# Lengths, lags and per-head shifts of a list schedule for attention, and twelve places for the value tiles

## The chip, the core and the metric

One core of a Trainium2 chip runs the whole kernel. Its engines are TensorE (PE in the profile, with PEld for its weight loads), VectorE (DVE), ScalarE (ACT), GpSimd (POOL) and SyncE (SP), which issues most of the DMAs. The metric is the device time of one execution in microseconds (us); several runs of a kernel are told by their median.

## The reference, cut to what matters

The kernel computes one layer of a transformer for 512 latent tokens and 256 context tokens: modulated RMS norms, two attention mixers side by side, an output projection and a gated feed-forward. The change lies in the attention. Its two mixers, eight heads each, are:

```python
def _diff_attend(q, k, v, lam):
    q1, q2 = jnp.split(q, 2, axis=-1)
    k1, k2 = jnp.split(k, 2, axis=-1)
    s1 = jnp.einsum('bhqd,bhkd->bhqk', q1, k1).astype(jnp.float32) * DA_SCALE
    s2 = jnp.einsum('bhqd,bhkd->bhqk', q2, k2).astype(jnp.float32) * DA_SCALE
    w = jax.nn.softmax(s1, axis=-1) - lam * jax.nn.softmax(s2, axis=-1)
    return jnp.einsum('bhqk,bhkd->bhqd', w.astype(v.dtype), v)

def _softmax_attend(q, k, v, scale):
    s = jnp.einsum('bhqd,bhkd->bhqk', q, k).astype(jnp.float32) * scale
    p = jax.nn.softmax(s, axis=-1)
    return jnp.einsum('bhqk,bhkd->bhqd', p.astype(v.dtype), v)
```

The first (differential attention) takes its queries, keys and values straight from the input projection `h @ w_in`. The second (latent attention) takes them from two normed latents, `c_q @ w_uq` and `c_kv @ w_ukv`. Keys and values come from all 768 tokens, queries from the 512 latent ones. The result of the first is normed per head, and both go through `w_o`.

## The kernel before, in words

All products are made of three matmuls each (helper `mm3`, lines 226 to 231): each operand is held as a rounded high part and the rest as a low part, and high x high, high x low and low x high are summed in PSUM. So every weight block and every intermediate is split: ScalarE casts the high part, VectorE subtracts it to get the low part (`split`, `parts`, `block`).

The stages in order of time are: norms and modulation; the input projection (features, then values); attention; the output projection; the feed-forward; the final norm.

**Values.** Lines 613 to 628 compute the values of all heads in two halves of 512 columns. Six PSUM tiles per half (`vo`, four in the two `s` tiles and two in `b` tiles) collect the products of sixteen k tiles. Each is then split into the tiles kh and kl of the pool `kvs`, two buffers for each tag, and stored to DRAM (`v_d`), by SP's queue in the first half and by POOL's in the second. In this stage the framework orders the instructions of the engines, and a gemv for the modulation (`next_gemv`) runs beside the products.

**Attention** is a flow (class `Flow`, line 73). Each piece of work is a `step` with an engine, a cost, a due time `at` and the buffers that it reads and writes; `lag` is the time from its end until another engine can use its result. `Flow.run` is a list scheduler: it goes through modelled time, and whenever an engine is free it takes, of the steps whose inputs are there and whose ring buffers are free, the one with the smallest `at`. Rings hand out their buffers in the order of `at`. The order found is then written out by hand for PE, ACT, DVE, SP and POOL; each engine executes its own list in order, and semaphores hold an instruction back until its inputs are there. The model's times have no other effect than this order.

- `SPANS` and `BASE` (742, 743) are the planned length and begin of the 16 heads, eight of each mixer, in us from the begin of attention.
- `da_feature` (808) makes the next head's queries: sixteen `mm3` into the tile f, the rotary embedding (`turned`) and the scaled split (`stacked`). Its weights come by `block` (652): a load by SP (`fetch`, 640) into a ring `wr` of three, due 14 before use, the cast `wh` and the rest `wl`. `hx_open` (892) follows the last feature.
- `scores` (686): four or ten matmuls into one of two `s` tiles, the negated row maximum `m` (DVE), exp into `p` with its sum (ACT).
- `weighted_values` (705): transposes of the weights (pt), their split into wth and wtl, and the product with the values in po.
- `load_keys`, `load_values`, the store of a head's output (`o_d`) and the weight blocks all go through SP's one queue.
- In the first mixer POOL scales the second softmax map and adds it to the first (841, 844).
- `open_latents` (868) frees the modulated input and loads the latents `cn` and the rotary key `krh` for the second mixer. `head_queries`, `head_keys`, `head_value` and `rotary_queries` make its operands; `sub_norm` (948) is the per-head norm of the first mixer's outputs, run beside the second.
- From line 1068 the first quarter of the output projection is in the same flow, so that it can stand among the last head's steps.

The pools `kv` and `kvs` of the projection are released before `dp` and `da` of attention are opened in the same SBUF. Lines 747 to 751 make some tiles ahead, to fix where the rings lie and with which buffer they begin.

The scheduler's lines on lags and choice:

```python
    LAGS = {"PE": 0.25, "ACT": 0.07, "DVE": 0.07, "POOL": 0.1, "SP": 3.5, "X": 0.0}
...
                    s = min(can, key=lambda s: (s.at, s.n))
```

Of the kernel before, what the change touches and what calls it, by code (L numbers as in the profile page):

```python
# [17 lines left out]
P = 128  # L18
D = 2048
KT = D // P  # L20
# [51 lines left out]

class Flow:


    LAGS = {"PE": 0.25, "ACT": 0.07, "DVE": 0.07, "POOL": 0.1, "SP": 3.5, "X": 0.0}

    def __init__(self):
        self.steps, self.rings = [], {}
# [6 lines left out]
    def step(self, eng, cost, at, fn, r=(), w=(), needs=(), lag=None):  # L86
        s = Step(eng, cost, self.LAGS[eng] if lag is None else lag, at, fn, len(self.steps))
# [22 lines left out]
    def run(self):  # L110
# [4 lines left out]
        engines = {e: now if e == "SP" else -3.0 for e in self.LAGS}  # L115
# [25 lines left out]
        event(-3.0)  # L141
# [36 lines left out]
def layer_kernel(ctx: ExitStack, tc: tile.TileContext, small, rope, c_row, cc_row, x_t, ctx_t, ada, ada_k,  # L178
# [457 lines left out]
    flow = Flow()  # L636
# [3 lines left out]
    def fetch(t, src, cols, lag=4.0):  # L640
# [8 lines left out]
        step("SP", 0.1 * len(src), t - 14, load, w=[raw], lag=lag)  # L649
        return raw  # L650

    def block(t, *src):
# [5 lines left out]
        step("ACT", 0.12 + cols * 0.00091, t - 4, lambda: sc.copy(hi()[:, :cols], raw()[:, :cols]), r=[raw], w=[hi])  # L658
        step("DVE", 0.15 + cols * 0.00104, t - 2.8, lambda: ve.tensor_tensor(
# [7 lines left out]
    def parts(t, hl, src, dst, of, scale=None, w=0.6, gap=0.7):  # L667
# [15 lines left out]
        step("DVE", w + 0.09, t + gap, second, r=[src, hl[0]], w=[hl[1]])  # L683


    def scores(t, cost, mms, reads, p, l, lcol, extra=None):
# [4 lines left out]
        def mm():  # L691
            ms = mms()
            for c0, c1 in ((0, T), (T, TT)):
# [4 lines left out]
        step("DVE", 0.95, t + cost + 0.2, lambda: ve.tensor_reduce(out=m(), in_=s()[:, :TT], axis=AX.X, op=ALU.max,  # L698
                                                                   negate=True), r=[s], w=[m])
        step("ACT", 1.1, t + cost + 1.3, lambda: sc.activation(p(), s()[:, :TT], AF.Exp, bias=m(), accum_out=lcol()),  # L700
             r=[s, m], w=[p, l])
# [3 lines left out]
    def weighted_values(t, pace, ws, v, vr, dst, after=None):  # L705

        po = buf(lambda: b_tile("po", 1), "po", 1)
        for kt in range(NKEY):
# [8 lines left out]
            step("PE", 0.44, t0, turn, r=ws, w=[pt])  # L717
            parts(t0 + 0.6, wt, pt, lambda b: b(), lambda pt=pt: pt())
            step("PE", 0.69, t0 + 2.5, lambda wt=wt, kt=kt: mm3(po(), v(kt), [b() for b in wt], kt == 0,
                                                                 kt == NKEY - 1), r=[*wt, *vr(kt)], w=[po])  # L720
        step("ACT", 0.6, t + pace * 5 + 3.4, lambda: sc.copy(dst(), po()), r=[po], w=[dst])
# [28 lines left out]
    da.tile([P, T], F32, tag="rt", name=nm("rt"), bufs=2)  # L750
    b_tile("pt", 2)
    zeroed = [buf(lambda t=t: t) for t in klz]
    for n_, (t, b) in enumerate(zip(klz, zeroed)):
        for i, r in enumerate((hi, lo)):
            step("SP", 0.1, FIRST + 3 * n_, lambda t=t, i=i, r=r: nc.sync.dma_start(t[r, i].bitcast(F32), zero_d), w=[b])
# [6 lines left out]
    def first_queries():  # L762
        qs = [da_buf([P, T], F32R, f"qs{i}", 2) for i in range(2)]
        for i in range(2):
            step("SP", 0.1, FIRST + 1, lambda i=i: nc.sync.dma_start(qs[i]().bitcast(F32), q0_d[i]), w=[qs[i]], lag=8.0)
        queries[0] = qs

    def load_keys(t, h):
# [7 lines left out]
        step("SP", 0.4, t, load, w=[ks, kl], lag=4.0 if h else 8.0)  # L776
        keys_[h] = ks, kl

    def load_values(t, h):
# [6 lines left out]
        step("SP", 0.2, t, load, w=hl)  # L786
        wvals[h] = hl

    def turned(t, src, tmp):

        q, u = tmp(), tmp()
        step("DVE", 0.69, t, lambda: ve.tensor_tensor(q(), src(), ropet[:, 0, :], op=ALU.mult), r=[src], w=[q])
        step("DVE", 0.75, t + 0.7, lambda: ve.stream_shuffle(u(), src(), mask=[i ^ 16 for i in range(32)]), r=[src],
             w=[u])
        step("DVE", 0.8, t + 1.5, lambda: ve.tensor_tensor(u(), u(), ropet[:, 1, :], op=ALU.mult), w=[u])
        step("DVE", 0.75, t + 2.3, lambda: ve.tensor_tensor(q(), q(), u(), op=ALU.add), r=[u], w=[q])
        return q

    def stacked(t, q, make, scale):
        qs = [make(i) for i in range(2)]  # L800
        for i, (r, o) in enumerate(((lo, hi), (hi, lo))):
            step("ACT", 0.63, t + 0.7 * i, lambda i=i, r=r: sc.mul(qs[i]()[r], q()[r], scale), r=[q], w=[qs[i]])
            step("DVE", 0.73, t + 0.7 * i + 0.8, lambda i=i, r=r, o=o: ve.scalar_tensor_tensor(
# [4 lines left out]
    def da_feature(f0, pace, h, blocks):  # L808
        f = buf(lambda: b_tile("f", 1), "f", 1)
        for kt in range(KT):  # L810
# [4 lines left out]
            step("PE", 0.69, f0 + pace * kt, mm, r=[*blocks[kt // 8], hx_open], w=[f])  # L815
# [14 lines left out]
    for h in range(NH):  # L830
        b, pace = BASE[h], SPANS[h] / 8
        ws = []
        for qt in range(NQT):
            ps = [weights_tile(), da_buf([P, TT], F32, "p1", 3)]
            l, rl = small("l", 2), small("rl", 2)
            for i in range(2):
# [3 lines left out]
            step("DVE", 0.17, t, lambda l=l, rl=rl: ve.reciprocal(rl(), l()), r=[l], w=[rl])  # L840
            step("POOL", 1.15, t + 0.2, lambda p=ps[1], rl=rl: gp.tensor_scalar(
                out=p(), in0=p(), scalar1=rl()[:, 1:2], scalar2=neglam, op0=ALU.mult, op1=ALU.mult), r=[rl], w=[ps[1]])
            step("ACT", 0.95, t + 0.2, lambda p=ps[0], rl=rl: sc.mul(p(), p(), rl()[:, 0:1]), r=[rl], w=[ps[0]])
            step("POOL", 1.9, t + 1.5, lambda ps=ps: gp.tensor_tensor(out=ps[0](), in0=ps[0](), in1=ps[1](),
                                                                      op=ALU.add), r=[ps[1]], w=[ps[0]])
            ws.append(ps[0])
        load_values(b + 2, h)
# [9 lines left out]
        hl = wvals[h]  # L857
        weighted_values(BASE[h + 1] + 4.0, 3.05, ws, lambda kt, hl=hl: [g()[:, kt * P:(kt + 1) * P] for g in hl],
# [959 lines left out]
```

## Time and profile before

| | |
|---|---|
| median of 3 runs | 2418.42 us (2418.08 to 2422.07) |
| the profiled execution, own time | 2417.74 us |
| its span, first to last instruction | 2416.0 us |
| mean granted TensorE clock | 0.994 |
| PE waits between 425 and 860 us | 18.3 us |

A row of the timeline has the start (us from the begin of the span), the length, engine, line, operation, the tile that is written and those that are read, the count, and in brackets how long the engine had been idle before it and what released it. In waits, the columns are the total, how often, and the longest. PE's lengths are modelled and overlap, since matmuls are pipelined; the pitch of two matmuls is read from their starts. A wait of an engine is idle time that ended with the event named.

### The profile page before, as it was taken

What the parts mean: (1) busy time and instruction counts of PE and PEld (TensorE: products, weight loads), DVE (VectorE), ACT (ScalarE), POOL (GpSimd) and SP (SyncE); (2) the same over time, 40 slices, a digit from 0 to 9 for tenths busy, and PEclk for the clock granted to TensorE, in tenths of its full rate; (3) what the DMA queues carried; (4) which work ended last, traced back from release to release, by engine and by line L of the source; (5) the groups of instructions that cost most, each with busy time, mean ns of one, the idle gap of its engine ahead of it and who ended that gap; (6) DMA issues with size and microseconds to landing.
All of it is one profiled execution on the core that took longest, in us unless ns stands there. A gap on an engine that the chain in (4) does not pass through costs nothing.

```text
span 2416.0 us, 33008 instructions
## 1 busy us (share of the span) xinstructions
PE 2345.0 (97%) x12758; PEld 1980.2 (82%) x12758; DVE 1698.2 (70%) x2244; ACT 1154.3 (48%) x1752; POOL 334.8 (14%) x320
## 2 busy tenths in 40 slices
PE   6999999999999999999999999999999999999998
PEld 3678888787788878888888888888888888888887
DVE  6668886387877777289575757676767676676667
ACT  4333121176776732255454545454544454554545
POOL 0000000154432222100101010101010111111110
PEclk9999999999999999999999999999999999999999
DMA  8867888734511168423555555555565656555563
GB/s 290 287 225 291 317 341 318 254 112 121 180 64 50 36 232 325 135 85 113 140 139 140 136 143 130 146 125 151 120 157 122 157 122 155 125 143 137 135 188 105
DMA packets 132852, 404.31 MB, mean 167 GB/s; under 512 B 14627, under 2 KB 25379, under 8 KB 124243
## 3 DMA queue, kind: packets, MB, share of 16 engines
q1 hardware_dynamic: 106166, 351.66, 44.0%
q0 software_dynamic: 25376, 49.49, 11.6%
q8 instruction: 100, 1.64, 0.3%
q10 hardware_dynamic: 1152, 1.05, 0.1%
q14 instruction: 58, 0.48, 0.1%
HBM read 332.47 MB, written 69.67 MB: 166 GB/s over the span
## 4 chain that ended last, share of the span: by engine, by line
PE 70%; issue 16%; DVE 6%; ACT 3%; DMA 2%; POOL 2%; SPq 0%; DVEq 0%; POOLq 0%; ACTq 0%
PE b L230 8%; PE b L229 8%; PE b L231 8%; PE y L1537 8%; PE z L1537 4%; PE y L1539 4%; PE s L229 4%; PE s L231 4%; PE s L230 4%; PE s L695 3%; PE z L1539 2%; POOL x_d L1558 2%; PE x L1537 1%; PE pt L715 1%; PE f L229 1%
## 5 line engine op out<-in xcount | busy, mean ns | idle before, releaser
L1558 POOL DMA_DIRECT2D x_d<-xs x160 | 139.8, 1003 | 1160.5 <-ACT xs L1557 1158.4
L1393 DVE TENSOR_TENSOR wl<-wr,wh 128x1024 fp32r<-128x1024 f32 x144 | 176.4, 1225 | 157.1 <-ACT wh L1385 156.5
L1385 ACT CAST wh<-wr 128x1024 fp32r<-128x1024 f32 x144 | 150.8, 1048 | 233.3 <-PE b L230 118.1
L229 PE MATMUL b<-ah,wh 128*128 128x512 f32 (+1 forms) x664 | 257.1, 387 | 0.0
L230 PE MATMUL b<-al,wh 128*128 128x512 f32 (+1 forms) x664 | 257.0, 387 | 0.0
L231 PE MATMUL b<-ah,wl 128*128 128x512 f32 (+1 forms) x664 | 256.2, 386 | 0.0
L1393 DVE TENSOR_TENSOR wl<-rb,wh 128x1024 fp32r<-128x1024 f32 x123 | 150.0, 1220 | 126.9 <-ACT wh L1385 126.9
L1385 ACT CAST wh<-rb 128x1024 fp32r<-128x1024 f32 x123 | 129.3, 1051 | 185.1 <-PE b L230 116.2
L1393 DVE TENSOR_TENSOR wl<-ws,wh 128x1024 fp32r<-128x1024 f32 x123 | 150.1, 1220 | 90.0 <-ACT wh L1385 90.0
L1385 ACT CAST wh<-ws 128x1024 fp32r<-128x1024 f32 x123 | 128.3, 1043 | 130.3 <-DVE ws L1347 44.5
L297 DVE CUSTOM_DVE_ANT_0 ada<-ada,cb,smt 128x2048 f32<-128x2048 f32 x64 | 152.1, 2381 | 40.7 <-DMA ada<-in_ada 40.4
L1537 PE MATMUL y<-a2k,wh 128*128 128x512 f32 x656 | 164.0, 392 | 0.0
L205 ACT CAST wh<-wr 128x1024 fp32r<-128x1024 f32 (+1 forms) x69 | 67.5, 978 | 178.8 <-PE b L231 76.3
L229 PE MATMUL b<-a2k,wh 128*128 128x512 f32 (+1 forms) x376 | 141.6, 377 | 5.9 <-ACT a2k L1242 4.3
L231 PEld LDWEIGHTS b<-ah,wl 128*128 128x128 f32 x664 | 124.9, 188 | 25.7
L229 PEld LDWEIGHTS b<-ah,wh 128*128 128x128 f32 x664 | 125.1, 188 | 22.8
L230 PEld LDWEIGHTS b<-al,wh 128*128 128x128 f32 x664 | 125.1, 188 | 21.9
L230 PE MATMUL b<-a2k,wh 128*128 128x512 f32 (+1 forms) x376 | 140.8, 374 | 0.0
L231 PE MATMUL b<-a2k,wl 128*128 128x512 f32 (+1 forms) x376 | 139.9, 372 | 0.0
L1537 PEld LDWEIGHTS y<-a2k,wh 128*128 128x128 f32 x656 | 118.7, 189 | 21.5
L206 DVE TENSOR_TENSOR wl<-wr,wh 128x1024 fp32r<-128x1024 f32 (+1 forms) x69 | 80.1, 1161 | 52.5 <-ACT wh L205 52.0
L698 DVE TENSOR_REDUCE m<-s 128x1 f32<-128x768 f32 x96 | 90.9, 950 | 28.1 <-PE s L695 27.9
(458 smaller groups left out, 5931.0 us busy)
## 6 DMA issues: line engine op xcount, KB each, us to landing
ada<-in_ada SPq DMA_DIRECT2D x64, 1024.0 KB, 6.2
rb<-in_w_up SPq DMA_DIRECT2D x123, 512.0 KB, 4.3
wr<-in_w_dn SPq DMA_DIRECT2D x88, 512.0 KB, 4.2
x_d<-xs POOLq DMA_DIRECT2D x160, 256.0 KB, 5.9
wr<-in_w_up SPq DMA_DIRECT2D x53, 512.0 KB, 4.2
wr<-in_w_f SPq DMA_DIRECT2D x34, 512.0 KB, 7.3
ada<-in_ada SPq DMA_DIRECT2D x32, 512.0 KB, 7.3
adak<-in_ada_k SPq DMA_DIRECT2D x32, 512.0 KB, 6.1
```

The lines of the kernel that those rows point to most:

```text
L206: ve.tensor_tensor(dst_l, src, dst_h.bitcast(F32), op=ALU.subtract)
L229: pe.matmul(out, st[0], mv[0], start=start, stop=False, **kw)
L230: pe.matmul(out, st[0], mv[1], start=False, stop=False, **kw)
L231: pe.matmul(out, st[1], mv[0], start=False, stop=stop, **kw)
L297: ve.tensor_tensor_reduce(out=junk, in0=w, in1=vec, op0=ALU.mult, op1=ALU.add, scale=1.0, scalar=col("b_ada", j), accum_out=dst[:, j:j + 1])
L695: pe.matmul(s()[:, c0:c1], a, b[:, c0:c1], start=i == 0, stop=i == len(ms) - 1)
L698: step("DVE", 0.95, t + cost + 0.2, lambda: ve.tensor_reduce(out=m(), in_=s()[:, :TT], axis=AX.X, op=ALU.max, negate=True), r=[s], w=[m])
L1385: sc.copy(t, raw[:, k * n_:k * n_ + n_])
L1393: ve.tensor_tensor(t, raw[:, k * n_:k * n_ + n_], hi[k].bitcast(F32), op=ALU.subtract)
L1537: pe.matmul(o, w[j][0], hs[j], start=start and j == 0, stop=False, skip_group_check=True)
L1539: pe.matmul(o[:, h0], w[j][1], hs[j][:, h0], start=False, stop=j == 7, skip_group_check=True)
L1558: gp.dma_start(x1_d[dt], x, accum_op=ALU.add)
```

## The change

It has two parts.

**Lengths, lags and shifts.** All costs in the flow are set anew, most a little shorter, POOL's longer, and DMA issues from 0.1 us apiece to about 0.4 to 0.6. The lag of a load goes from 3.5 or 4.0 to 6.0, and loads are due 16 instead of 14 before use. A table `PLAN` shifts the due times of named groups of steps: s0 to s15 are the scores of the 16 heads, f1 to f7 a head's loads and the next head's features, w0 to w15 the weighted values, m the second mixer's queries and keys, v its values, n the sub-norms, x the opening of pools, o the projection. Due times of the features and of the latents' loads move, and the engines begin at different times.

```diff
+PLAN = {
+    "f1": -1.5, "f2": -3.2, "f3": -0.3, "f4": 1.2, "f5": -0.3, "f6": -2.3, "f7": -20.4, "m-1": 2.0, "m0": 3.2,
...
+    0.2, "w12": -2.7, "w13": 2.2, "w14": 0.3, "w15": 10.3, "x": 4.8}
...
-    LAGS = {"PE": 0.25, "ACT": 0.07, "DVE": 0.07, "POOL": 0.1, "SP": 3.5, "X": 0.0}
+    LAGS = {"PE": 0.2, "ACT": 0.14, "DVE": 0.14, "POOL": 0.1, "SP": 6.0, "X": 0.0}
...
     def step(self, eng, cost, at, fn, r=(), w=(), needs=(), lag=None):
+        at += self.plan.get(self.part, 0.0)
...
-        engines = {e: now if e == "SP" else -3.0 for e in self.LAGS}
+        engines = {"PE": -3.0, "ACT": 2.0, "DVE": 2.8, "POOL": 0.0, "SP": now, "X": -3.0}
...
-    def fetch(t, src, cols, lag=4.0):
+    def fetch(t, src, cols, lag=6.0):
...
-        step("SP", 0.1 * len(src), t - 14, load, w=[raw], lag=lag)
+        step("SP", 0.5 * len(src), t - 16, load, w=[raw], lag=lag)
...
-        step("ACT", 1.1, t + cost + 1.3, lambda: sc.activation(p(), s()[:, :TT], AF.Exp, bias=m(), accum_out=lcol()),
-             r=[s, m], w=[p, l])
+        step("ACT", 0.9, t + cost + 1.2, lambda: sc.activation(p(), s()[:, :TT], AF.Exp, bias=m(), accum_out=lcol()),
+             r=[s, m], w=[p, l], lag=0.25)
...
-        step("SP", 0.4, t, load, w=[ks, kl], lag=4.0 if h else 8.0)
+        step("SP", 2.4, t, load, w=[ks, kl], lag=6.0)
...
-            f0, fp = (-3.0, 0.85) if h == 0 else (b - 5, (SPANS[h] - 4) / 16)
+            f0, fp = (-3.0, 0.85) if h == 0 else (11.5 + 21.6 * (h - 1), 1.15)
...
-    step("X", 0.0, BASE[7] - 4.5, lambda: None, w=[hx_open])
-    step("SP", 1.1, BASE[7] - 4.5, open_latents, r=[hx_open], w=[latent_open, krs[0]], lag=12.0)
+    step("X", 0.0, BASE[7] - 17, lambda: None, w=[hx_open])
+    step("SP", 4.5, BASE[7] - 17, open_latents, r=[hx_open], w=[latent_open, krs[0]], lag=9.0)
...
-            f = b + (7 if p else 3.5)
+            f = b + (7 if p else 0.0)
...
-        sub_norm(b + 7, h)
+        sub_norm(b + 4, h)
```

**The values' places.** The twelve copies of a half go to twelve entries: six tiles of a ring v, three tiles of the pool kv that the norm of the latents had used, and three tiles of the ring again. The copies get a high priority in the framework's order. The second half collects its first two token tiles in the `b` banks and, in its last k tile, takes the `s` banks first. Four buffers of the ring p0 are made ahead.

```diff
-        vo = [s0[:, :512], s0[:, 512:], s1[:, :512], s1[:, 512:], b0, b1_]
+        vo = [s0[:, :512], s0[:, 512:], s1[:, :512], s1[:, 512:]]
+        vo = [b0, b1_, *vo] if half else [*vo, b0, b1_]
...
-                for t in range(NKEY):
+                order = (2, 3, 4, 5, 0, 1) if half and kt == KT - 1 else range(NKEY)
+                for t in order:
...
-        for t in range(NKEY):
-            for i, g in enumerate(split_tiles(kvs, ("kh", "kl"), [P, 4, P], 2, vo[t].rearrange("p (h d) -> p h d", h=4))):
+        if not half:
+            kvs.release()
+            kvs = tc.alloc_tile_pool(name="kv2", bufs=6, reuse_waits="tile")
+        homes = [(kvs, "v", 6)] * 6 + [(kv, g, 1) for g in ("nq", "nr", "n1")] + [(kvs, "v", 6)] * 3
+        for t in order:
+            hl = []
+            for _ in range(2):
+                pool, g, bufs = homes.pop(0)
+                hl.append(pool.tile([P, 4, P], F32R, tag=g, name=nm(g), bufs=bufs))
+            with tc.high_priority():
+                split(*hl, vo[t].rearrange("p (h d) -> p h d", h=4))
+            for i, g in enumerate(hl):
                 (nc.sync, gp)[half].dma_start(v_d[half][:, :, i, t].rearrange("h p d -> p h d"), g.bitcast(F32))
...
+    for _ in range(4):
+        weights_tile().make()
```

More of the change, by code (lines that the diff above doesn't have):

```diff
@@ L140, in run @@
         event(now)
-        event(-3.0)
+        for t in set(engines.values()):
+            event(t)
         while events:
@@ L682, in parts @@
         step("ACT", w, t, first, r=[src], w=[hl[0]])
-        step("DVE", w + 0.09, t + gap, second, r=[src, hl[0]], w=[hl[1]])
+        step("DVE", w * 1.25, t + gap, second, r=[src, hl[0]], w=[hl[1]])
     def scores(t, cost, mms, reads, p, l, lcol, extra=None):
@@ L954, in sub_norm @@
         f = buf(lambda: b_tile("f", 1), "f", 1)
-        step("SP", 0.1, t, lambda: nc.sync.dma_start(o(), o_d[h]), r=[o_ready[h], out_open], w=[o])
-        step("ACT", 0.65, t + 3.7, lambda: sc.square(q(), o()), r=[o], w=[q])
-        step("ACT", 0.6, t + 4.4, lambda: sc.copy(qh(), q()), r=[q], w=[qh])
-        step("POOL", 1.3, t + 5, lambda: gp.tensor_tensor(out=ql(), in0=q(), in1=qh().bitcast(F32), op=ALU.subtract),
+        step("SP", 0.4, t, lambda: nc.sync.dma_start(o(), o_d[h]), r=[o_ready[h], out_open], w=[o])
@@ L959, in sub_norm @@
+        step("ACT", 0.65, t + 6.7, lambda: sc.square(q(), o()), r=[o], w=[q])
+        step("ACT", 0.53, t + 7.3, lambda: sc.copy(qh(), q()), r=[q], w=[qh])
+        step("POOL", 1.3, t + 8, lambda: gp.tensor_tensor(out=ql(), in0=q(), in1=qh().bitcast(F32), op=ALU.subtract),
              r=[q, qh], w=[ql])
-        step("PE", 0.46, t + 7, lambda: [pe.matmul(f(), onesr, g(), start=i == 0, stop=i == 1)
+        step("PE", 0.455, t + 9.6, lambda: [pe.matmul(f(), onesr, g(), start=i == 0, stop=i == 1)
@@ L970, in sub_norm @@
-        step("POOL", 0.75, t + 12, lambda: gp.tensor_scalar(out=t2(), in0=t2(), scalar1=-0.5, scalar2=1.5,
+        step("ACT", 0.52, t + 11.6, lambda: sc.activation(rs(), rs(), AF.Exp, scale=-0.5), w=[rs])
+        step("ACT", 0.55, t + 12.2, lambda: sc.mul(o(), o(), subs), w=[o])
+        step("POOL", 1.15, t + 12.2, lambda: gp.tensor_tensor(out=t2(), in0=rs(), in1=rs(), op=ALU.mult), r=[rs], w=[t2])
+        step("POOL", 1.4, t + 13.4, lambda: gp.tensor_tensor(out=t2(), in0=t2(), in1=s1(), op=ALU.mult), r=[s1], w=[t2])
@@ L975, in open_outputs @@
+        step("POOL", 1.4, t + 17.5, lambda: gp.tensor_tensor(out=o(), in0=o(), in1=rs(), op=ALU.mult), r=[rs], w=[o])
     def open_outputs():
```

94 lines of the change are left out of this document (52 added, 42 removed), and 5 rows, old and new, of the table PLAN.

## The prediction, made before the changed kernel ran

> **What bounds the kernel now.** I read the page first: busy shares and the chain of work that ended last.
>
> ```profile
> PE 2345.0 (97%) x12758; PEld 1980.2 (82%) x12758; DVE 1698.2 (70%) x2244; ACT 1154.3 (48%) x1752; POOL 334.8 (14%) x320
> ...
> PE 70%; issue 16%; DVE 6%; ACT 3%; DMA 2%; POOL 2%; SPq 0%; DVEq 0%; POOLq 0%; ACTq 0%
> ```
>
> TensorE does the work and the chain runs on it, so the change can win only where TensorE stands still in the part that it touches, and lose only by adding such places. Next, busy time by stretch; the columns are length, then busy us (and count) of PE, PEld, DVE, ACT and POOL, then granted clock, DMA share and GB/s.
>
> ```profile
> 558.20:584.90 26.70, 24.79 (x120) 20.00 (x120) 17.69 (x25) 15.65 (x29) 9.76 (x8) 0.95 0.43 124
> 584.90:612.00 27.10, 26.50 (x128) 21.60 (x129) 21.68 (x31) 19.94 (x35) 13.26 (x9) 0.94 0.41 122
> ...
> 640.00:664.00 24.00, 19.23 (x98) 14.73 (x97) 22.73 (x33) 18.12 (x34) 11.55 (x9) 1.00 0.62 216
> ...
> 853.70:870.00 16.30, 16.30 (x81) 13.55 (x80) 10.27 (x16) 7.63 (x12) 0.00 (x0) 1.00 0.36 118
> 880.00:920.00 40.00, 40.00 (x179) 33.12 (x177) 32.73 (x28) 10.37 (x12) 9.41 (x7) 1.00 0.94 355
> ```
>
> Attention runs from its first feature product at 473 (part one) to about 854. Behind it TensorE is busy for 16.30 of 16.30 and 40.00 of 40.00 us: what attention saves reaches the end, as long as the DMA share of 0.94 there does not become a bound, which it is not today. Then, TensorE's waits, the first row from 380 to 425 us and the others from 425 to 860 us (total, times, longest):
>
> ```profile
> PE s L229 <- DVE kl L206: 1.1, 1, 1.1
> ...
> PE s L695 <- ACT p L700: 9.3, 8, 2.2
> PE pt L715 <- DVE wtl L678: 5.3, 6, 3.2
> PE po L230 <- DVE wtl L678: 2.1, 3, 1.6
> PE pt L715 <- DVE p L1022: 0.6, 1, 0.6
> PE s L229 <- DVE vl L678: 0.5, 1, 0.5
> PE f L229 <- DVE rt L793: 0.5, 1, 0.5
> ```
>
> 1.1 + 9.3 + 5.3 + 2.1 + 0.6 + 0.5 + 0.5 = 19.4 us in 21 waits: the whole pool, beside what a wait costs after it.
>
> **The change, part one: the values' evictions.** Today six PSUM tiles per half are copied through rings of two (kh, kl), so each copy waits until the store two before has landed.
>
> ```profile
> 415.32 0.47 PE L229 MATMUL s<-wh,a2k 128*128 128x512 f32 x1 [1.14 <-DVE kl L206]
> ...
> 473.24 0.39 PE L229 MATMUL f<-a2k,wh 128*128 128x512 f32 x1
> ...
> 477.84 0.59 ACT L205 CAST kh<-b 128x512 fp32r<-128x512 f32 x1 [1.29 <-DMA v_d<-kh]
> ...
> 481.10 1.81 DVE L698 TENSOR_REDUCE m<-s 128x1 f32<-128x768 f32 x2
> ...
> 483.13 0.50 PE L695 MATMUL s<-ks,qs 128*128 128x512 f32 x1 [2.18 <-ACT p L700]
> ...
> 486.32 0.98 POOL L841 TENSOR_SCALAR p<-p,rl,neglam 128x768 f32<-128x768 f32 x1 [4.09 <-DVE rl L840]
> ...
> 500.08 0.50 PE L695 MATMUL s<-ks,qs 128*128 128x512 f32 x1 [0.87 <-ACT p L700]
> ...
> L628 POOL DMA_DIRECT2D v_d<-kh x6: 750/750/790, 471.6 to 480.5; - x6
> v_d<-kh POOLq DMA_DIRECT2D x6, 256.0 KB, 2.6
> ```
>
> At 477.84 ScalarE still waits for a store (2.6 us from issue to landing); VectorE, in order, reaches the first maximum only at 481.10, so exp is late and TensorE stops for 2.18 us at 483.13. Likewise 1.14 us at the boundary of the halves. Twelve copies into nine tiles (the last three take the first three again, whose stores are by then the oldest) need 6 x 0.59 us on ScalarE and about as much on VectorE, beside matmuls. The second half also starts in the free b banks, which puts two tiles' matmuls ahead of the reused s banks, and ends with the s banks, which the scores need first. I count 1.14 + 2.18 gone and half of 0.87: **3.7 us**. Bounds 0 and 4.2. The stores stay twelve a half on the same two queues (SP, then POOL at 0.75 us each); POOL's first softmax step comes behind 4.09 us of idle, so they delay nothing there. But three tiles of the kv pool are now held until their stores land. By the pools' sizes they lie at 25 to 34 KB of a partition, under the first slots of the p0 ring (24 to 48 KB); the four tiles made ahead turn that ring, so that the slots used first lie behind them. Cost nothing; without that cover the first exp would wait for the stores, 12 x 0.75 + 2.6 = 11.6 us after the first copy instead of some 5, so about 6 us.
>
> **Part two: the late weight blocks.** New lengths, shifts and lags give another order on each of five queues; no instruction is added or taken away.
>
> ```profile
> 545.08 0.58 SPq L860 DMA_DIRECT2D o_d<-o  x1
> 545.75 2.51 SPq L646 DMA_DIRECT2D wr<-in_w_f  x2
> 554.32 1.05 ACT L658 CAST wh<-wr 128x1024 fp32r<-128x1024 f32 x1 [4.39 <-DMA wr<-in_w_f]
> ...
> 554.33 0.39 PE L230 MATMUL f<-a2k,wh 128*128 128x512 f32 x1
> 554.56 0.40 PE L231 MATMUL f<-a2k,wl 128*128 128x512 f32 x1
> 558.14 1.12 PE L715 MATMUL pt<-ident,p 128*128 128x128 f32 x4 [3.19 <-DVE wtl L678]
> ...
> 575.75 0.38 SPq L646 DMA_DIRECT2D wr<-in_w_f  x1
> 582.84 1.04 ACT L658 CAST wh<-wr 128x1024 fp32r<-128x1024 f32 x1 [3.70 <-DMA wr<-in_w_f]
> 584.83 0.76 PE L695 MATMUL s<-ks,qs 128*128 128x512 f32 x1 [1.91 <-ACT p L700]
> ...
> wr<-in_w_f SPq DMA_DIRECT2D x11, 512.0 KB, 7.3
> ```
>
> The old list takes 0.1 us for an issue and 4.0 until it lands. The chip took 554.32 - 545.75 = 8.6 and 582.84 - 575.75 = 7.1 us, 7.3 in the median. So ScalarE came to the cast too early and stood for 4.39 and 3.70 us with exp and the splits queued behind it; TensorE stopped for 3.19 and 1.91 us, and ran at a granted 0.95 and 0.94 for 26.7 and 27.1 us (second fence): (1 - 0.95) x 26.7 + (1 - 0.94) x 27.1 = 3.0 us more. The new list takes 0.5 + 6.0 = 6.5 us, and asks two us earlier (t - 16). That still falls 0.8 us short of the median and 2.1 of the worst, but not the 3.2 and 4.5 of today. Two score tiles ahead cover such a rest. I count 3.19 + 1.91 + 3.0 = 8.1 less 1.1 that stays: **7.0 us**. Bounds 0 and 8.1.
>
> **Part three: the change from the first attention to the second.**
>
> ```profile
> 637.68 2.70 SPq L876 DMA_DIRECT2D cn<-cq_d  x6
> 640.42 2.17 SPq L876 DMA_DIRECT2D cn<-ckv_d  x4
> ...
> PE s L695 <- ACT p L700: 4.3, 5, 1.7
> ```
>
> The last row is TensorE's wait for exp between 640 and 665 us. VectorE is busy for 22.73 of 24 us there, and TensorE has no other work: the latents that feed the second attention are fetched only at 637.68, after the last feature product. Now each head's features start earlier (due 11.5 + 21.6 (h - 1) instead of 12 + 23.2 (h - 1): 8.5 us for h = 6, the last, and 2.3 more by its shift), and the latents' ten loads and the rotary key's go to 17 instead of 4.5 before head 7. On SP's queue they pass head 7's keys and values and the first w_ukv, w_uqr and w_uqn blocks, which can come later by the 2.70 + 2.17 us that these issues take; what waits for those are casts due 12 us after their loads. TensorE then has the second attention's query and key products while exp catches up. VectorE's load is spread, not lowered, so I take 3.5 of 4.3: **3.5 us**, bounds 0 and 4.3.
>
> **Part four: the rest.** 19.4 - 4.2 - 5.1 - 4.3 = 5.8 us in small waits through the second attention and at its end, where the last head's values now come 10.3 later among the projection's products. They have no single cause, and a list in true lengths should halve them: **2.9 us**, bounds 0 and 5.8. The sub-norm's earlier loads and longer POOL lengths lie beside TensorE's work: nothing, and if that cover went, their result is first read at the output split some 10 us on.
>
> A stop also costs its refill: two products start 0.23 us apart (554.33, 554.56); from 554.56 to 558.14 are 3.58 us, and 3.58 - 0.23 - 3.19 = 0.16. With 14 of 21 waits gone that is **2.2 us**, bounds 0 and 3.4.
>
> Against it stand new stops, since an order made for fixed lengths meets jitter in other places. The nearest row is a wait for exp of 9.3 / 8 = 1.2 us; I take two to three, **-3.0 us**, bounds 0 and -9.3 (as many as now).
>
> Sum: 3.7 + 7.0 + 3.5 + 2.9 + 2.2 - 3.0 = 16.3 us. The profiled execution took 2417.7 us by its own time (span 2416.0), 0.7 under the median of 2418.4: 2417.7 - 16.3 = 2401.4, at the median about **2402 us**.
>
> **The rivals.** *First, the lengths do not hold.* One length per operation is put into the list, yet these rows differ from themselves (mean of the group; then min/median/max of the line):
>
> ```profile
> L659 DVE TENSOR_TENSOR wl<-wr,wh 128x1024 fp32r<-128x1024 f32 x16 | 22.5, 1406 | 9.7 <-ACT wh L658 9.5
> L1078 DVE TENSOR_TENSOR a2k<-or,a2k 128x512 fp32r<-128x512 f32 x15 | 13.3, 923 | 0.7 <-ACT a2k L1076 0.7
> ...
> L659 DVE TENSOR_TENSOR wl<-wr,wh x33: 680/1225/2766, 484.0 to 886.2; 128x1024 fp32r<-128x1024 f32 x21, 128x896 fp32r<-128x896 f32 x4, 128x768 fp32r<-128x768 f32 x4, 128x512 fp32r<-128x512 f32 x4
> ...
> L1078 DVE TENSOR_TENSOR a2k<-or,a2k x16: 675/682/1783, 841.7 to 868.0; 128x512 fp32r<-128x512 f32 x16
> ```
>
> VectorE lost (1.406 - 1.225) x 16 + (0.923 - 0.682) x 15 = 6.5 us in two groups, all with both inputs in SBUF. If a tighter order puts that whole loss, now partly beside idle time, before a maximum or a split, the gain is 16.3 - 6.5 = 9.8: **2408 us**. For it: the spread up to 2.77 us. Against: both groups together are 31 instructions. The Trainium skill's page "SBUF — State Buffer", section "Who interferes with whom", names a cause that a list of fixed lengths cannot hold: a VectorE instruction with two SBUF inputs and a GpSimd instruction that reads SBUF exclude each other, and the later one waits for the whole of the other. By that rule each hit costs up to one POOL addition and comes and goes with the order; the spread in these rows agrees with it, without proving it.
>
> *Second, only the evictions count:* the list's waits move instead of going. For it: the list before was also made with lengths and still left 15 us of waits. Gain 3.7 and a little refill: **2414 us**.
>
> *Third, slower: SP's queue.* A block's load stands behind a store that waits for ScalarE (545.08 before 545.75), and the lag of 6.5 is under the 7.3 measured. One block that comes too late cost 3.19 + (1 - 0.95) x 26.7 = 4.5 us. Should the new order leave six such blocks of the twelve w_f loads instead of two, it gives 3.7 + 3.5 + 2.9 + 2.2 - 3.0 = 9.3 us and takes 4 x 4.5 = 18: **2427 us**; from five (13.5) on it is slower. Against it: with the shorter lag of today only two of eleven stopped ScalarE visibly.
>
> **How the numbers follow.** Forecast 0.66 (own range 2391 to 2410: every wait, the clock and the refill gone is 19.4 + 3.0 + 3.4 = 25.8; half the gain is 8), first rival 0.12, second 0.10, third 0.12. This kernel's measurements tell 0.2% (4.8 us) from no change: faster means under 2413.6, slower over 2423.2. The forecast and the first rival are faster, and a fifth of the second: 0.80. The rest of the second is within: 0.08; the third is slower: 0.12. The range runs from 2391 to 2419, up to the second rival and the no-change value above it; it leaves out the third and a little at the low end.
>
> **What would show it.** Right: no wait of copies for v_d stores and a first maximum 3 to 5 us after 473 instead of 8; no cast of a w_f block that stands over 2 us, the granted clock 1.00 from 530 to 612; the cn loads well before head 7's scores; TensorE's waits in attention at 5 to 9 us. Wrong: new stops of TensorE behind a wr load, VectorE's two-input means rising, or waits of over 14 us in other places.

## The result, and the profile after

The changed kernel took 2404.76 us (median of 6 runs, 2401.39 to 2406.75) beside 2419.51 us for the kernel before on the same chip. The medians lie 14.8 us apart; the ratio, estimated from all runs, is 0.9931, with a 95% interval of 0.9915 to 0.9948, so about 17 us less. Run again beside later experiments on another chip (c1_changed) it came to 0.9917, 0.9906 to 0.9929. Its profiled execution took 2404.97 us, span 2403.1. Line numbers below are those of the changed kernel: 12 to 40 higher than before; other runs have their own, a few lines off. Busy shares, after:

```profile
PE 2342.3 (97%) x12758; PEld 1981.3 (82%) x12758; DVE 1701.1 (71%) x2244; ACT 1153.6 (48%) x1752; POOL 336.3 (14%) x320
```

The same instructions and nearly the same busy time: the gain is idle time of TensorE. Attention from its first feature product to the first product of the next projection, two rows of TensorE's timeline:

```profile
475.67 0.39 PE L241 MATMUL f<-a2k,wh 128*128 128x512 f32 x1
...
881.63 0.39 PE L241 MATMUL b<-a2k,wh 128*128 128x512 f32 x1
```

That is 406.0 us. The same two rows stood at 473.24 and 895.74 before, 422.5 us. So attention is 16.5 us shorter; it began 2.4 us later in this execution, and what lies behind it took 2403.1 - 881.63 = 1521.5 us beside 2416.0 - 895.74 = 1520.3 before. What attention saved did reach the end. TensorE's waits from 425 to 862 us (total, times, longest):

```profile
PE po L242 <- DVE wtl L702: 4.3, 3, 1.8
PE pt L739 <- DVE wtl L702: 1.9, 2, 1.5
PE f L241 <- DVE rt L819: 0.3, 1, 0.3
PE s L719 <- ACT p L724: 0.2, 1, 0.2
PE s L241 <- ACT p L724: 0.2, 1, 0.2
```

6.9 us in 8 waits, where 19.4 us in 21 were. The waits for exp, 9.3 us before, are 0.4; what is left is nearly all for wtl, the low half of the weights, which VectorE makes. The first three stretches of the prediction's second fence, after:

```profile
558.00:584.90 26.90, 24.31 (x124) 20.24 (x125) 22.41 (x32) 18.57 (x33) 13.55 (x9) 1.00 0.44 141
584.90:612.00 27.10, 27.10 (x139) 22.65 (x138) 23.36 (x32) 20.65 (x36) 13.72 (x9) 1.00 0.34 85
640.00:664.00 24.00, 22.56 (x115) 19.11 (x115) 20.13 (x32) 18.22 (x35) 11.51 (x8) 0.93 0.20 60
```

The granted clock is 1.00 in the first two, where it was 0.95 and 0.94. From 640 to 664 TensorE is busy for 22.56 instead of 19.23 us, but at 0.93. The first row holds two stops that are new, at 558.81 and 567.31. Here is what stands ahead of the three new stops; the rows of VectorE, GpSimd and TensorE are put together in order of time:

```profile
555.76 1.85 POOL L871 TENSOR_TENSOR p<-p,p 128x768 f32<-128x768 f32 x1
555.80 2.36 DVE L821 TENSOR_TENSOR rt<-rt,ropet 128x512 f32<-128x512 f32 x1
558.08 0.68 DVE L702 TENSOR_TENSOR wtl<-pt,wth 128x512 fp32r<-128x512 f32 x1
558.81 0.50 PE L242 MATMUL po<-wtl,vh 128*128 128x512 f32 x1 [1.06 <-DVE wtl L702]
...
561.87 1.88 POOL L868 TENSOR_SCALAR p<-p,rl,neglam 128x768 f32<-128x768 f32 x1 [4.26 <-DVE rl L867]
562.91 3.62 DVE L829 SCALAR_TENSOR_TENSOR qs<-rt,qs 64x512 fp32r<-64x512 f32 x2
563.83 2.15 POOL L871 TENSOR_TENSOR p<-p,p 128x768 f32<-128x768 f32 x1
...
567.31 0.50 PE L242 MATMUL po<-wtl,vh 128*128 128x512 f32 x1 [1.78 <-DVE wtl L702]
...
638.02 1.84 POOL L871 TENSOR_TENSOR p<-p,p 128x768 f32<-128x768 f32 x1 [0.20 <-POOL p L868]
638.09 2.72 DVE L683 TENSOR_TENSOR wl<-wr,wh 128x896 fp32r<-128x896 f32 x1
...
641.46 0.64 PE L242 MATMUL po<-wtl,vh 128*128 128x512 f32 x1 [1.44 <-DVE wtl L702]
```

Each time a VectorE instruction with both operands in SBUF comes while one of GpSimd's runs, and it ends only about its own length after that one (of the pair at 562.91 it is the second, which meets the addition at 563.83); wtl stands behind it in VectorE's queue, and TensorE stops. The same rotary product that lasts 2.36 us here lasts 0.69 where GpSimd is idle:

```profile
625.99 0.69 DVE L821 TENSOR_TENSOR rt<-rt,ropet 128x512 f32<-128x512 f32 x1
```

This is the rule of the Trainium skill that the first rival drew on ("SBUF — State Buffer", section "Who interferes with whom"): the later of the two waits for the whole of the other. The rows agree to within 0.14 us: GpSimd's addition ends at 555.76 + 1.85 = 557.61, and 557.61 + 0.69 = 558.30, where the product's row ends at 555.80 + 2.36 = 558.16. It goes the other way too: GpSimd's scaling at 561.87 came while VectorE's rest wl ran (561.68 to 562.88), and took 1.88 us, where the median of its line is 0.99.

### The profile page after: what moved, and what is told of

It reads as the page before. It is cut to its first block, busy times and chain, and to the rows that moved or that the text cites. A ratio compares the mean times of both kernels' runs of the same rounds, so it can differ in the third digit from the quotient of the medians.

```text
span 2403.1 us, 33008 instructions
## 1 busy us (share of the span) xinstructions
PE 2342.3 (97%) x12758; PEld 1981.3 (82%) x12758; DVE 1701.1 (71%) x2244; ACT 1153.6 (48%) x1752; POOL 336.3 (14%) x320
## 4 chain that ended last, share of the span: by engine, by line
PE 84%; DVE 7%; DMA 4%; ACT 3%; issue 2%; SPq 0%; DVEq 0%; ACTq 0%
PE y L1577 12%; PE b L242 10%; PE b L241 10%; PE b L243 9%; PE z L1577 6%; PE y L1579 6%; PE s L241 3%; PE s L719 3%; PE s L243 3%; PE s L242 3%; PE z L1579 3%; DMA ada<-in_ada 3%; PE x L1577 2%; PE f L241 1%; PE f L242 1%
```

## The experiments

The theory at first: the terms of the prediction are real and add up, evictions and list apart, each part of the list by its own waits; and the three new stops are two engines in each other's way. Rivals: the parts only work together; the stops belong to the order. After the first runs the question was narrowed to what in the list earns the gain, its lengths or its shifts.

Times by ratio to the kernel before, run on the same chip; 0.001 is 2.4 us. "Attention" is the time in the profiled execution from the last product before attention to the first product behind it, by TensorE's timeline (0.2 us more than above). It is given because the stage before attention varies: its end lay between 471.1 and 481.7 us in executions of kernels with one and the same code there, and whole times carry that. It comes from one execution of each kernel; the two of the changed kernel differ by 0.8 us.

| kernel | median us | ratio, interval | attention us |
|---|---|---|---|
| before | 2419.5 to 2422.2 | 1 | 422.7 |
| changed | 2404.76 | 0.9931, 0.9915 to 0.9948 | 406.2 |
| c1_changed | 2401.62 | 0.9917, 0.9906 to 0.9929 | 407.0 |
| e1_values | 2416.82 | 0.9980, 0.9969 to 0.9992 | 420.5 |
| e2_schedule | 2406.06 | 0.9935, 0.9922 to 0.9947 | 406.2 |
| e4_pool_short | 2393.30 | 0.9881, 0.9867 to 0.9896 | 398.3 |
| e7_port | 2399.06 | 0.9908, 0.9895 to 0.9920 | 403.9 |
| e5_dma_times | 2422.40 | 1.0005, 0.9995 to 1.0014 | 423.3 |
| e3_no_shifts | 2411.89 | 0.9962, 0.9949 to 0.9975 | 419.1 |
| e6_late_latents | 2415.79 | 0.9974, 0.9963 to 0.9984 | 419.2 |
| e10_old_search | 2400.40 | 0.9912, 0.9897 to 0.9927 | 402.1 |
| e11_other_shifts | 2410.34 | 0.9951, 0.9939 to 0.9962 | 412.2 |
| e9_port_search | 2399.58 | 0.9908, 0.9895 to 0.9921 | 404.3 |
| e12_port_search2 | 2400.74 | 0.9910, 0.9897 to 0.9922 | 404.2 |

**Each half of the change alone.** e1_values keeps the list of before and takes only the twelve places, the order of the halves and the four p0 tiles; e2_schedule takes only the list.

```diff
 e2_schedule
-        vo = [b0, b1_, *vo] if half else [*vo, b0, b1_]
+        vo = [*vo, b0, b1_]
...
-        homes = [(kvs, "v", 6)] * 6 + [(kv, g, 1) for g in ("nq", "nr", "n1")] + [(kvs, "v", 6)] * 3
...
-    for _ in range(4):
-        weights_tile().make()
```

> The kernel before with the values' twelve places, the half order and the four p0 tiles alone; the list of attention stays the old one. Theory (each part gives what its waits of TensorE cost): the waits of 1.14, 2.18 and 0.87 us go, 4 us less, 2415.5 us, ratio 0.998 to before. Rival (the old list was made for engines that come free late, and waits further on take the gain back): no change, 2419.5 us, the same sum of TensorE waits further on.

> The changed kernel with the values evicted as before (kh and kl rings of two); lengths, lags, shifts and due times of the new list stay. Theory (the parts add up): the waits around 415 and 480 us come back, 4 us more than the changed kernel, some 2409 us, ratio 0.9955. Rival (the new list counts on ScalarE and VectorE being free 2 to 3 us after its begin, so both parts need each other): 2412 us or more, with waits also in heads 1 and 2.

> The changed kernel unaltered, for comparison on the same chip with the three beside it: ratio 0.993 to before.

The places alone bring 0.0020, 4.8 us (1.9 to 7.5), as forecast. The list alone brings 0.0065, so that the two add up to 0.0085, a little above both measurements of the whole (0.0069 and 0.0083), within their intervals. e2 was forecast at 0.9955; at 0.9935 it is not shown to be slower than the changed kernel. In its trace the stop at the boundary of the halves is back, in two waits from 380 to 425 us:

```profile
PE s L241 <- DVE kl L218: 4.8, 2, 2.9
```

That the old places cause it is not shown. e10_old_search below has the twelve places, and TensorE stops there for longer, behind a step of the modulation's gemv that waits for its load at the head of VectorE's queue (in order of time):

```profile
412.24 2.35 DVE L310 CUSTOM_DVE_ANT_0 ada<-ada,cb,smt 128x2048 f32<-128x2048 f32 x1 [3.53 <-DMA ada<-in_ada]
...
417.08 0.76 PE L242 MATMUL s<-wh,a2k 128*128 128x512 f32 x1 [5.63 <-DVE v L219]
```

In e11_other_shifts, with the twelve places too, it is 4.61 us behind such a step, and in e2 itself the gemv waits 3.39 us for its load ahead of the first of the two waits. Attention in e2 is as long as in the changed kernel, though e1 alone shortens it by 2.2 us: with the new list the places show no gain inside attention. The list is by far the larger half.

**GpSimd's steps shortened.**

```diff
 e4_pool_short
-                out=p(), in0=p(), scalar1=rl()[:, 1:2], scalar2=neglam, op0=ALU.mult, op1=ALU.mult), r=[rl], w=[ps[1]])
+                out=p()[:, :8], in0=p()[:, :8], scalar1=rl()[:, 1:2], scalar2=neglam, op0=ALU.mult, op1=ALU.mult), r=[rl], w=[ps[1]])
```

> The changed kernel with POOL's two steps of the first mixer's softmax (scaling the second map, adding it to the first) done on 8 of 768 columns; the list and its order stay. This leaves out the rest of the second map's part in the weights. Theory (the three long waits for wtl at 559, 567 and 641 us come from VectorE instructions with two SBUF inputs that stand while POOL's addition reads SBUF): the waits of 1.06, 1.78 and 1.44 us go, the clock stays at 1.00 after 641, VectorE's rotary product and query rests take 0.69 and 0.70 us throughout: 4.3 us and some 2 us of clock less, 2399 us. Rival (the order itself lets wtl come late): the waits stay where they are, 2404 to 2405 us.

TensorE's waits in attention, of this kernel:

```profile
PE pt L739 <- DVE wtl L702: 1.9, 2, 1.5
PE f L241 <- DVE rt L819: 0.3, 1, 0.3
PE s L241 <- ACT p L724: 0.2, 1, 0.2
```

Its stretch from 640 to 664 us, columns as above:

```profile
640.00:664.00 24.00, 24.00 (x135) 20.61 (x134) 20.33 (x36) 19.79 (x39) 2.66 (x8) 1.00 0.23 76
```

And one group of its VectorE (count, then busy us, mean ns):

```profile
L829 DVE SCALAR_TENSOR_TENSOR qs<-rt,qs 64x512 fp32r<-64x512 f32 x14 | 9.7, 692 | 0.4
```

The three new stops are gone and the others stay (the two waits of pt for wtl at 1.9), apart from one of 0.2 us for exp. The clock is back at 1.00, and qs lasts 692 ns where the changed kernel has this row:

```profile
L829 DVE SCALAR_TENSOR_TENSOR qs<-rt,qs 64x512 fp32r<-64x512 f32 x14 | 13.5, 966 | 0.4
```

Attention is 8.7 us shorter than in c1_changed, more than the 6 us forecast. The list's order was not touched, so the cause of the three stops is shown: the two engines' shared access, not the order by itself. The 8.7 us are not the price of that access alone, since GpSimd's sums also come earlier here.

**The list told of that access.** In e7_port a VectorE step with two operands in SBUF is not started while a GpSimd step runs, nor the other way round; lengths and shifts stay.

```diff
 e7_port
+                    can = [s for s in open_[e] if s.ready <= now + 1e-9 and all(free(b) for b in s.takes)
+                           and not (s.port and held[other[e]] > now + 1e-9)]
```

> The changed kernel whose list scheduler knows one rule more: a VectorE step with two SBUF inputs and a POOL step of attention are not started while the other runs; all lengths and shifts stay. Theory (exclusion of the two is what the fixed lengths miss): TensorE's waits for wtl at 559, 567 and 641 go without work being cut, 2398 to 2402 us. Rival (the exclusion costs nothing that matters, or keeping the two apart delays POOL's sums and the splits as much): 2404 to 2412 us, with new waits for p or wtl.

Attention falls by 3.1 us against c1_changed; the whole times differ by 0.0009, inside the intervals. The median lies in the theory's range, but so does that of c1_changed, so the whole time decides nothing. The long waits for wtl are fewer (po 1.1 us in one wait).

**One part of the list undone at a time.** e5_dma_times gives DMA issues and latencies of before back to the new list (but for the latents' loads), e3_no_shifts empties the table of shifts, e6_late_latents gives the due times of features and latents back.

```diff
 e5_dma_times
-    LAGS = {"PE": 0.2, "ACT": 0.14, "DVE": 0.14, "POOL": 0.1, "SP": 6.0, "X": 0.0}
+    LAGS = {"PE": 0.2, "ACT": 0.14, "DVE": 0.14, "POOL": 0.1, "SP": 3.5, "X": 0.0}
...
-        step("SP", 0.5 * len(src), t - 16, load, w=[raw], lag=lag)
+        step("SP", 0.1 * len(src), t - 14, load, w=[raw], lag=lag)
 e3_no_shifts
-    flow = Flow(PLAN)
+    flow = Flow({})
 e6_late_latents
-            f0, fp = (-3.0, 0.85) if h == 0 else (11.5 + 21.6 * (h - 1), 1.15)
+            f0, fp = (-3.0, 0.85) if h == 0 else (b - 5, (SPANS[h] - 4) / 16)
...
-    step("X", 0.0, BASE[7] - 17, lambda: None, w=[hx_open])
+    step("X", 0.0, BASE[7] - 4.5, lambda: None, w=[hx_open])
```

> The changed kernel with the loads' times of the old list (issue 0.1 us apiece, 4.0 us to land, weight blocks due 14 us before use); lengths of the engines, shifts and due times stay new. Theory (what ended the two late blocks is the true landing time in the list): casts of w_f blocks stand again on ScalarE for 2 to 4 us, TensorE stops once or twice behind them and the clock falls: 5 to 8 us more than the changed kernel, ratio 0.995 to 0.9965. Rival (the features' earlier due times alone bring the loads early enough): same as the changed kernel, 0.993, no cast that waits over 1 us.

> The changed kernel with the table of shifts empty; lengths, lags, due times and value places stay new. Theory (true lengths and lags carry the gain, the shifts the small waits of the second mixer): 3 to 6 us more than the changed kernel, ratio 0.9945 to 0.9955, the added waits mostly behind 665 us. Rival one (the shifts carry it): ratio 0.998, as with the evictions alone. Rival two (the shifts do nothing on the chip): 0.993.

> The changed kernel with the features' due times, the latents' loads (4.5 us before head 7) and the first block of the second mixer as in the list before; all else new. Theory (early latents give TensorE work while exp catches up at the change of mixers): latents land some 10 us later, waits of 2 to 4 us for exp come back there, ratio 0.9945. Rival (TensorE stands there for VectorE's rotary work and the splits whatever the loads do): within 1 us of the changed kernel, 0.993, with waits for wtl or exp of the same sum.

Each of the three loses most of the gain: attention is 12 to 16 us longer than in c1_changed. By whole time e3 loses a little over half of it, 0.0045 of 0.0083, e6 0.0057, and e5 all; the execution of e3 that gave its attention was the slowest of its five. No forecast gave the size: e5 and e6 lost some two to four times what theory said, and e3, at 0.9962, lies between the theory and its first rival. In e5 ScalarE's casts wait for blocks of weights again, and TensorE for exp:

```profile
ACT wh L682 <- DMA wr<-in_w_f: 13.1, 4, 5.1
ACT wh L682 <- DMA wr<-in_w_uqr: 3.6, 1, 3.6
...
PE s L719 <- ACT p L724: 10.6, 5, 3.7
```

In e6 there is no such place; small waits are spread over all of attention (the largest groups):

```profile
PE po L242 <- DVE wtl L702: 4.5, 7, 1.3
PE f L241 <- DVE qnl L704: 2.7, 2, 2.5
PE s L719 <- ACT p L724: 2.7, 5, 1.2
```

And e3, with the new lengths and latencies but no shifts, is only 1.4 us of attention better than e1, which has the old ones and no shifts; with the new latencies its casts still wait 5.6 us for w_f blocks. So these parts are not terms that can be added; either shifts need true lengths, or shifts only need to be made for the lengths they stand with. The next runs tell these apart.

**Old lengths with shifts of their own; another table for the new lengths.** e10_old_search is e1_values with a table sought for the old lengths and the engines' new begin times; e11_other_shifts is the changed kernel with another table.

```diff
 e10_old_search (against the changed kernel)
-    LAGS = {"PE": 0.2, "ACT": 0.14, "DVE": 0.14, "POOL": 0.1, "SP": 6.0, "X": 0.0}
+    LAGS = {"PE": 0.25, "ACT": 0.07, "DVE": 0.07, "POOL": 0.1, "SP": 3.5, "X": 0.0}
...
-    "f1": -1.5, "f2": -3.2, "f3": -0.3, "f4": 1.2, "f5": -0.3, "f6": -2.3, "f7": -20.4, "m-1": 2.0, "m0": 3.2,
+    "f0": 2.3, "f1": 0.9, "f2": -4.3, "f3": -4.1, "f4": -3.0, "f5": -3.1, "f6": -7.8, "f7": 8.3,
```

> The values' places of the changed kernel, but the list with the lengths, the latencies of loads and the due times of before; only the shifts by part are there, sought anew so that the list's own forecast of attention falls from 410.0 us (no shifts, these lengths) to 394.4 (the changed kernel's list forecasts 391.7 with its lengths). Theory: shifts pay only as far as the lengths are those of the chip, above all the loads', which the list thinks land in 3.5 to 4 us; the order is fitted to times that do not occur, and most of the 16 us of the forecast is lost: 2410 to 2420 us, ratio 0.996 to 1.000, with ScalarE's casts waiting for loads of weights again by 5 us or more in all. Rival: the shifts alone earn the gain, whatever the lengths: 2400 to 2406 us, ratio 0.992 to 0.994.

> The changed kernel with another set of shifts and nothing else: one that its own list, with the same lengths, forecasts 2.3 us shorter than the changed kernel's (389.5 against 391.7 us of attention). Rival: the list with the trace's lengths tells the chip's time, so this kernel is 1 to 3 us faster than the changed one, ratio 0.990 to 0.992. Theory: the list leaves out that VectorE's instructions with two operands in SBUF and GpSimd's stand in each other's way. An estimate from replaying both orders, each engine in its own order, with these kept apart: 404.7 us for the changed kernel, whose trace shows 406, and 418 for this one, so it is 13 us slower than the changed kernel: about 2414 us, ratio 0.995 to 0.999, with TensorE's waits behind VectorE's weights (wtl) twice the 5 us of the changed kernel or more.

The theory falls in e10. With the lengths and latencies of before and shifts made for them, the kernel is as fast as the changed one (0.9912), and its attention is the shortest of all whole ones, 402.1 us. What the engines' begin times alone do was not run. No cast waits for a block of weights (0.3 us, where the same list without shifts had 7.4), although the list still counts 4 us for a load. The largest of TensorE's waits, and that of ScalarE:

```profile
PE po L243 <- DMA klz<-kr_d: 1.7, 1, 1.7
PE po L243 <- DVE wtl L703: 1.2, 2, 0.9
...
ACT wh L683 <- DMA wr<-in_w_f: 0.3, 1, 0.3
```

e11 goes as the theory said and not as the list said: the list counts it 2.3 us shorter, and the chip took 0.9951, 0.0034 or 8 us more than c1_changed, attention 5.2 us more. The size is less than the 13 us of the estimate, and waits for wtl rose from 6.9 us (c1_changed: 5.0 for po, 1.9 for pt) to 9.7, not to twice that:

```profile
PE po L243 <- DVE wtl L703: 7.2, 6, 2.8
PE pt L740 <- DVE wtl L703: 2.5, 2, 1.9
```

Two of these stops in the timeline of the three engines, in order of time:

```profile
686.57 1.29 POOL L1003 TENSOR_TENSOR sr<-sr,s 128x512 f32<-128x512 f32 x1
686.58 1.82 DVE L822 TENSOR_TENSOR rt<-rt,ropet 128x512 f32<-128x512 f32 x1
687.94 1.61 POOL L1004 TENSOR_TENSOR or<-or,sr 128x512 f32<-128x512 f32 x1
688.44 1.66 DVE L823 TENSOR_TENSOR rt<-rt,rt 128x512 f32<-128x512 f32 x1
...
690.76 0.50 PE L243 MATMUL po<-wtl,vh 128*128 128x512 f32 x1 [1.55 <-DVE wtl L703]
...
847.91 3.69 DVE L1119 TENSOR_TENSOR a2k<-or,a2k 128x512 fp32r<-128x512 f32 x6
...
852.26 0.49 PE L243 MATMUL po<-wtl,vh 128*128 128x512 f32 x1 [2.78 <-DVE wtl L703]
```

The stop at 690.76 is the shared access again. The longest one, at 852.26, is not: six subtractions of 0.6 us each, none stretched, stand ahead of wtl in VectorE's queue. Three lists' own forecasts of attention now stand beside the chip's: 394.4 and 402.1 us in e10, 391.7 and 406 to 407 in the changed kernel, 389.5 and 412.2 in e11. The shorter the forecast, the longer the attention.

**A version meant to beat both.** e9_port_search and e12_port_search2 are e7_port with GpSimd's first softmax step at its undisturbed length and tables sought with the two engines kept apart.

```diff
 e9_port_search (against e7_port)
-            step("POOL", 1.85, t + 0.2, lambda p=ps[1], rl=rl: gp.tensor_scalar(
+            step("POOL", 1.0, t + 0.2, lambda p=ps[1], rl=rl: gp.tensor_scalar(
...
-    "f1": -1.5, "f2": -3.2, "f3": -0.3, "f4": 1.2, "f5": -0.3, "f6": -2.3, "f7": -20.4, "m-1": 2.0, "m0": 3.2,
+    "f0": 2.1, "f1": -4.3, "f2": 2.6, "f3": 1.5, "f4": 4.0, "f5": -1.7, "f6": 1.5, "f7": -4.3, "m-1": -16.7,
```

> The changed kernel whose list does not start a VectorE step with two operands in SBUF while one of GpSimd's runs (nor the other way round), with GpSimd's first softmax step at 1.0 us, as the trace has it where it runs alone, in place of 1.85, and with shifts sought anew for this list, replayed with the two kept apart. An estimate from that replay: 391 us of attention against 404.7 for the changed kernel. Theory: the port is what the changed kernel's list lacked, so this kernel is 8 to 14 us faster than the changed one: 2388 to 2394 us, ratio 0.986 to 0.9885, no wait of TensorE for wtl over 1 us, and granted clock 1.00 from 620 to 670 us. Rival: an order is one draw, and no list finds a better one by design: within 5 us of the changed kernel, 2397 to 2407 us, ratio 0.990 to 0.994.

> As the run before it, with another set of shifts that the same replay puts at the same 391 us. Theory: the same time as its twin within 3 us, 2388 to 2394 us, ratio 0.986 to 0.9885. Rival (an order is one draw): the twins lie 5 us or more apart.

The twins agree (0.9908 and 0.9910, attention 404.3 and 404.2), 2 us below c1_changed and inside its interval: the rival's bound, not the theory's 8 to 14 us. That the twins lie together speaks against the rival's reason, that each order is a draw. The replay had put their attention at 391 us, 13 too short. The list keeps the two engines apart by its own clock, and nothing holds the chip to that clock. In e9 they still meet, here VectorE's four subtractions, 2.5 us where they run alone, beside the sub-norm of GpSimd:

```profile
833.79 5.81 DVE L1123 TENSOR_TENSOR a2k<-or,a2k 128x512 fp32r<-128x512 f32 x4
...
835.76 1.61 POOL L1007 TENSOR_TENSOR sr<-sr,s 128x512 f32<-128x512 f32 x1
...
840.26 0.50 PE L247 MATMUL po<-wtl,vh 128*128 128x512 f32 x1 [1.56 <-DVE wtl L707]
```

No version that does the whole work is shown to be faster than the changed kernel: the intervals overlap. That the engines could be held apart by waits on one another was not tried.

## Why the prediction was right

The time came out 3 us above the 2402 forecast, inside the range, and the sum of 16.3 us stands beside 16.5 us in attention's trace. The likeliest case was the right one: TensorE's waits in attention went, and what went reached the end. Term by term the sum was less good than its total, and that the total fits so well is luck: one term is 2.4 us too low, another's price 3.0 too low.

- **Part one, 3.7 us.** The 1.14 and 2.18 us are gone and 0.87 became 0.19: 4.0 us. e1 alone gives 4.8 (1.9 to 7.5), but e2 has the same attention without the places, so the 2.18 and 0.68 inside it do not add to what the list wins; and the stop at the boundary came in e10 and e11 in spite of them. Copies still wait for stores, against the sign named (ScalarE 1.11 us at 413.51). "Cost nothing" for the cover of the p0 ring was wrong in its reason: ScalarE's first exp does wait for a store of the pool kv, while TensorE has the first features to do. The first maximum came 3.4 us after the first feature, as forecast:

```profile
479.05 0.95 DVE L722 TENSOR_REDUCE m<-s 128x1 f32<-128x768 f32 x1
...
481.75 0.90 ACT L724 ACTIVATE p<-s,m 128x768 f32<-128x768 f32 x1 [2.69 <-DMA v_d<-nq]
```

- **Part two, 7.0 us.** Both stops of 3.19 and 1.91 us and the lower clock are gone, all of 8.1. That this comes from latencies of 6.5 us in the list, as the prediction put it, is the step that failed. e5 and e10 refute it together: with these shifts the old latencies bring the waits back, with other shifts they do not, and in e3 the new latencies without shifts leave 5.6 us of them.
- **Part three, 3.5 us.** The prediction left out that the table's x shifts the latents' loads back by 4.8 of the 12.5 us. They are issued 14 us earlier all the same, and the 4.3 us for exp are gone; 1.49 and 0.44 us remain for wtl, since VectorE now does the last features' rotary ahead of it. Some 2.4 us net.

```profile
623.90 2.70 SPq L905 DMA_DIRECT2D cn<-cq_d  x6
...
629.08 0.63 PE L739 MATMUL pt<-ident,p 128*128 128x128 f32 x4 [1.49 <-DVE wtl L702]
```

- **Part four, 2.9 us, and refills, 2.2 us.** The small waits fell from 5.8 to 0.5 us, nearly twice the forecast; 13 waits fewer at 0.16 us are 2.1.
- **New stops, -3.0 us.** Three, as forecast, of 1.06, 1.78 and 1.44 us, 4.3 in all, and (1 - 0.93) x 24 = 1.7 us of clock behind the last: 6.0, twice the price. Their cause is not jitter in general but the first rival's mechanism; without most of GpSimd's work there (e4) attention is 8.7 us shorter. VectorE's two-input means rising was named as a sign of being wrong, and some rose: wl of 1024 columns from 1363 to 1448 ns, qs from 852 to 966; a2k fell from 908 to 707.

Measured terms: 4.0 + 8.1 + 2.4 + 5.3 + 2.1 - 6.0 = 15.9, of which 1.1 lies ahead of attention; the other 1.7 of the 16.5 are not assigned to a place. **The rivals:** the first has the right mechanism, but it took its share out of a larger gain (2408 was forecast for it). The second, that waits only move, falls: e2 brings 0.0065 without the evictions. The third, a late load on SP's queue, did not come about here; e5 shows its mechanism, 16.7 us of casts that wait, and it takes the time only back to that of before (1.0005), not past it.

## What to carry to other kernels

The waits in a trace can tell what a new order may win, but not which of its knobs wins it: shifts, lengths and due times of a list act together, and taking one away cost 12 to 16 of the 16 us of attention each time, 11 to 21 of 20 us in whole time. Judge an order on the chip, not by the list's own length: one that the list counted 2.3 us shorter ran 5 us longer in attention and 8 in all. True lengths were not needed where the shifts were sought for the lengths in use (e10). Telling the list of the two engines that exclude each other won 3 us of attention, none of it clear of the noise in whole times; whether waits that hold the planned order between the queues would win more is open.

## What the hardware showed unexpectedly

A stop of TensorE can cost its clock as much time again, and the same stop need not. In the changed kernel TensorE stood for 1.44 us up to 641.46, and the clock was granted at 0.53 over the next 3.5 us. In the second execution of the same kernel (c1_changed) the same stop of 1.44 us ended at 639.49 and lowered nothing; there the clock fell behind the stop of 1.80 us that ended at 562.94, whose like in the first, 1.78 us up to 567.31, had lowered nothing (1.00 from 558 to 584.9). The first row is of the changed kernel, the others are of c1_changed, columns as above:

```profile
641.46:645.00 3.54, 3.54 (x10) 2.85 (x11) 3.54 (x5) 1.86 (x4) 2.47 (x2) 0.53 0.00 0
...
639.49:643.50 4.01, 4.01 (x19) 3.36 (x20) 3.65 (x5) 2.76 (x6) 2.94 (x2) 1.00 0.06 11
...
562.94:567.00 4.06, 4.06 (x14) 3.25 (x15) 3.06 (x5) 2.88 (x6) 0.99 (x1) 0.62 0.03 6
```

From 641.46 to 644.89 nine products ran, seven of 512 columns and two of 256. At the pitches of 0.23 and 0.12 us beside them they would have taken 1.85 us; they took 3.43, so 1.6 us went to the clock, more than to the stop. In e2_schedule, with the same list, there are stops of 1.02, 1.75 and 1.45 us and the clock stays at 1.00 behind them all. So neither the length of a stop nor its place in the program decides it alone, and what does is open. The 3.0 us of clock in the prediction's part two are to be read with this: run again, the changed kernel has 0.94 over 27 us from 554 on.
